# Token-major k, q and v of a gated-delta mixer by VectorE block transposes and scattered stores

## The chip, the cores and the metric

The kernel runs on one NeuronCore of one Trainium2 chip. The metric is the device time of one execution in microseconds; a lower number is better. The kernel before took 2305.7 us (median of 3 runs, 2305.63 to 2308.47).

The engines are named as the profile names them: PE (TensorE, matrix products) with its weight loads PEld, DVE (VectorE), ACT (ScalarE), POOL (GpSimd) and SP (SyncE, whose queue issues every DMA of this kernel). Each engine works through its own instructions in a fixed order and waits where an operand is not there yet.

## The reference

One layer of a hybrid encoder trunk, on a prompt of 2048 tokens and a sample of 32, width 1024, all in fp32:

- h = RMSNorm(x) with shift and scale from a conditioning vector, then one input projection whose columns feed two mixers.
- Mixer A: u and v through GELU, v normalised and mixed over 128-token chunks, out = u * (W v + b).
- Mixer B, the gated delta rule, is where the change lies. For each of 4 heads of 128 features:

```
qkv = silu(causal_conv(qkv, width 4))
q = l2norm(q) * 128 ** -0.5 ;  k = l2norm(k)
beta = sigmoid(b) ;  g = -exp(a_log) * softplus(a + dt_bias)
S_t = a_t S_{t-1} (I - b_t k_t k_t^T) + b_t v_t k_t^T ;  o_t = S_t q_t
```

  evaluated in chunks: a triangular system per chunk, products of q and k inside the chunk, and a state S of 128 x 128 that is carried from chunk to chunk.
- The mixers' outputs are joined and projected, added to x with a gate; then a feed-forward block of width 4096 with squared ReLU, and a final RMSNorm. Besides y, the last conv rows and the states S are returned.

## The kernel before

**Precision and layout.** A large product is three fp32r products of high and low parts (`mm3`): `BH`, `BL` are the parts of the activations, `wh`, `wl` those of the weights. Activations lie feature-major: 128 features on the partitions, tokens along the row. The prompt is worked in two halves (`hf`): 1024 tokens in two groups of 512, and 1056 tokens (with the sample) in groups of 384, 384 and 288.

**Stages of a half** (`mixers`, from about 90 us to 970 us): the v columns and gates of mixer A and the decays; then six weight slabs of two 128-column tiles each for k, q and v of the heads (z too in the second half); then u; then the output projection. During the first half's k/q/v slabs, `x_stats(1)` also makes the normalised input of the second half, with 48 loads of x and 24 stores and loads of h1.

**A k, q or v tile** (`qkv_tile`, L1146): each group accumulates 24 products in a bank of the ring `g`, ACT copies the bank to `raw`, DVE makes the conv with three more multiply-adds from `raw`, ACT applies SiLU, and the result is stored feature-major to DRAM: `kq_d` for k and q, `v_d` for v.

**A head** (`delta_local`, L1183) follows its v tile. For each pair of chunks (256 tokens, four pairs a half) it loads `kq` (ring `kq1`, slot 7) and `vt`, transposes k and q of both chunks on PE into a bank of the ring `L`, squares them on ACT with an accumulated sum for the norms, and copies k, scaled by the decay `ekg`, into the packet `pk`; POOL makes the power -1/2 of four sums. PE makes the products k with k and q in a second bank `L`, DVE multiplies them with the decays: one result goes to `pk`, the other stays as the triangular system. v is transposed in a third bank `L`, scaled and copied to `pk`, and `pk` (3 x 256 columns) is stored. `delta_inv` then inverts the triangular systems of two heads, and `delta_chain` runs the state over the eight chunks of two heads, loading `pk`, the inverse `us` and `kq` a pair ahead.

**What sets the order.** No order is written out by hand. Every operation is recorded with an engine, a cost, a class (chain, inversion, local work, evacuation, large product) and what it depends on, and `Program.schedule` places operations one at a time, engine by engine, by class and due time. On PE the large products fill the time in which smaller work is not ready. The outcome is a fixed list for each engine, in which nothing overtakes. A DMA's planned cost comes from its bytes; the argument `n` of `dma` gives another number of bytes to plan with.

**Helper lines.** Since helpers record everything, the profile's lines are those of the helpers: L358 activations, L373 `tt`, L378 `stt`, L387 `ts`, L396 copies, L404 the 32 x 32 block transpose of DVE, L411 every DMA, L420 every product, L431 every PE transpose. The tiles tell them apart: `g`, `L`, `C`, `B`, `M`, `f` are PSUM banks, `s` is any of the 28 SBUF slots. Names in the trace leave out digits, so `s<-kq_d` is a load of any head.

## Time and profile before

| | |
|---|---|
| median of 3 runs | 2305.7 us |
| profiled execution, its own time | 2305.26 us |
| profiled execution, its span from the first to the last instruction | 2303.5 us |
| mean granted clock of PE | 0.998 |
| PE busy, 180 to 980 us | 795.0 of 800 us |
| DMA busy share, whole span | 72.6% in the one queue that SP issues to |
| DMA traffic | 547 MB, 238 GB/s mean |

Feed-forward work fills the time from about 985 us on; the mixers with their projections lie before. In the first half the k/q/v tiles run from about 180 to 340 us, in the second from about 470 to 700 us. A busy PE in these views includes overlap between neighbouring instructions: starts tell how fast they follow each other.

### The profile page before, as it was taken

How to read it: one execution, taken by the hardware profiler on the slowest of the kernel's cores; microseconds unless marked ns; L12 is line 12 of the kernel's file. 1: busy time of each engine (PE TensorE's matmuls, PEld its weight loads, DVE VectorE, ACT ScalarE, POOL GpSimd, SP SyncE). 2: the span in 40 equal slices, each digit the busy share in tenths (PEclk: the TensorE clock that was granted, in tenths of full speed). 3: DMA queues.
4: the chain of work that ended last, by engine and by line, in shares of the span. 5: the costliest groups of instructions: out<-in, count | busy, mean ns of one | idle time of the engine just before them, and what ended most of it. 6: DMA issues, size and time to landing. Idle time of an engine off the chain costs nothing.

```text
span 2303.5 us, 45375 instructions
## 1 busy us (share of the span) xinstructions
PE 2280.8 (99%) x15890; PEld 2172.0 (94%) x15890; DVE 1660.0 (72%) x3599; ACT 1208.3 (52%) x2787; POOL 568.0 (25%) x722
## 2 busy tenths in 40 slices
PE   9999999999999999999999999999999999999998
PEld 6877879999999988999999999999999999999998
DVE  7556756677654546589999989876668885666775
ACT  5466656566654434476655546753444564344344
POOL 1123531222413023444445424210001250000001
PEclk9999999999999999999999999999999999999999
DMA  9578877576556857987777787997668797666771
GB/s 330 170 267 285 265 233 234 154 225 206 155 182 197 263 190 226 295 267 265 257 255 263 251 273 242 335 306 246 216 212 265 258 306 230 217 220 216 249 221 54
DMA packets 358198, 547.32 MB, mean 238 GB/s; under 512 B 66233, under 2 KB 182093, under 8 KB 357969
## 3 DMA queue, kind: packets, MB, share of 16 engines
q1 hardware_dynamic: 357968, 544.42, 72.6%
q8 instruction: 125, 2.05, 0.4%
q14 instruction: 105, 0.85, 0.1%
HBM read 390.96 MB, written 153.31 MB: 236 GB/s over the span
## 4 chain that ended last, share of the span: by engine, by line
PE 84%; DVE 6%; DMA 4%; ACT 2%; issue 2%; SPq 1%; POOL 1%; POOLq 0%; DVEq 0%; ACTq 0%
PE f L420 47%; PE g L420 27%; DVE s L373 4%; PE C L420 3%; PE B L420 2%; PE L L420 2%; DVE wl L373 1%; SPq L411 1%; ACT s L358 1%; PE M L420 1%; PE L L431 1%; DMA s<-x_d 1%; POOL s L373 0%; DMA s<-s_d 0%; ACT wh L358 0%
## 5 line engine op out<-in xcount | busy, mean ns | idle before, releaser
L420 PE MATMUL f<-s,wh 128*128 128x348 f32 (+1 forms) x2768 | 662.3, 322 | 1.3 <-DVE s L373 1.3
L358 ACT ACTIVATE s<-s 128x348 f32<-128x348 f32 (+13 forms) x1059 | 491.2, 487 | 326.6 <-DVE s L373 146.8
L420 PEld LDWEIGHTS f<-s,wh 128*128 128x128 f32 x2768 | 481.0, 188 | 3.3 <-DVE s L373 2.8
L373 DVE TENSOR_TENSOR s<-f,s 128x348 f32<-128x348 f32 (+1 forms) x696 | 348.0, 513 | 166.6 <-PE f L420 164.5
L420 PE MATMUL f<-s,wl 128*128 128x348 f32 (+1 forms) x1384 | 444.7, 321 | 0.0
L420 PE MATMUL g<-BH,wh 128*128 128x384 f32 (+2 forms) x1088 | 400.4, 368 | 2.4 <-ACT s L358 1.9
L373 DVE TENSOR_TENSOR s<-s,s 128x348 fp32r<-128x348 f32 (+8 forms) x674 | 353.2, 553 | 41.1 <-ACT s L358 20.5
L420 PE MATMUL g<-BH,wl 128*128 128x384 f32 (+2 forms) x1088 | 381.7, 351 | 0.0
L420 PE MATMUL g<-BL,wh 128*128 128x384 f32 (+2 forms) x1088 | 380.6, 350 | 0.5 <-DVE BL L378 0.5
L420 PE MATMUL f<-BL,wh 128*128 128x348 f32 (+1 forms) x1024 | 330.2, 322 | 0.0
L420 PE MATMUL f<-BH,wh 128*128 128x348 f32 (+1 forms) x1024 | 329.0, 321 | 0.0
L420 PE MATMUL f<-BH,wl 128*128 128x348 f32 (+1 forms) x1024 | 328.6, 321 | 0.0
L373 POOL TENSOR_TENSOR s<-s,s 128x512 f32<-128x512 f32 (+17 forms) x303 | 241.3, 800 | 341.2 <-ACT s L358 138.0
L358 ACT ACTIVATE wh<-s 128x512 fp32r<-128x512 f32 x282 | 176.6, 631 | 226.6 <-PE f L420 180.3
L420 PEld LDWEIGHTS f<-s,wl 128*128 128x128 f32 x1384 | 260.4, 188 | 0.0
L373 DVE TENSOR_TENSOR wl<-s,wh 128x512 fp32r<-128x512 f32 x282 | 217.2, 777 | 37.9 <-ACT wh L358 37.7
L420 PEld LDWEIGHTS g<-BH,wh 128*128 128x128 f32 x1088 | 204.9, 188 | 26.8 <-issue 7.1
L420 PEld LDWEIGHTS g<-BH,wl 128*128 128x128 f32 x1088 | 204.3, 188 | 18.2
L420 PEld LDWEIGHTS g<-BL,wh 128*128 128x128 f32 x1088 | 205.4, 189 | 16.6 <-DVE BL L378 0.8
L378 DVE SCALAR_TENSOR_TENSOR s<-s,s,s 128x256 f32<-128x256 f32 (+4 forms) x314 | 164.1, 544 | 55.3 <-ACT s L358 29.5
L358 ACT ACTIVATE wh<-wr 128x512 fp32r<-128x512 f32 (+2 forms) x159 | 124.3, 783 | 139.6 <-PE f L420 61.0
L420 PEld LDWEIGHTS f<-BL,wh 128*128 128x128 f32 x1024 | 192.3, 188 | 0.4 <-DVE BL L373 0.3
(134 smaller groups left out, 3264.6 us busy)
## 6 DMA issues: line engine op xcount, KB each, us to landing
s<-w_u SPq DMA_DIRECT2D x124, 256.0 KB, 3.6
s<-w_d SPq DMA_DIRECT2D x121, 256.0 KB, 3.9
wh<-su_d SPq DMA_DIRECT2D x114, 256.0 KB, 3.8
wl<-su_d SPq DMA_DIRECT2D x114, 256.0 KB, 4.1
wh<-sd_d SPq DMA_DIRECT2D x100, 256.0 KB, 3.0
wl<-sd_d SPq DMA_DIRECT2D x100, 256.0 KB, 3.8
wr<-w_b SPq DMA_DIRECT2D x36, 512.0 KB, 5.0
s<-adaw SPq DMA_DIRECT2D x32, 512.0 KB, 5.9
```

The lines of the kernel that those rows point to most:

```text
L358: self.p.op(ACT, c, lambda: nc.scalar.activation(out=R(out), in_=R(in_), func=func, **{k: R(v) for k, v in kw.items()}), [out, accum], [in ...
L373: self.p.op(eng, c, lambda: e.tensor_tensor(out=R(out), in0=R(a), in1=R(b), op=op), [out], [a, b])
L378: self.p.op(DVE, c, lambda: nc.vector.scalar_tensor_tensor(out=R(out), in0=R(a), scalar=R(s), in1=R(b), op0=op0, op1=op1), [out], [a, s, b])
L411: self.p.op(DMA, max(500, x), lambda: nc.sync.dma_start(out=R(out), in_=R(in_)), [out], [in_], lat=LAND + b / RATE - max(500, x))
L420: nc.tensor.matmul(R(out), R(l), R(r), **kw)
L431: self.p.op(PE, 114, lambda: nc.tensor.transpose(R(out), R(in_), R(ident)), [out], [in_, ident])
```

## The change

k, q and v of a tile are no longer transposed by PE. After the SiLU of a whole tile, kept in one buffer `yo` of 1056 columns, DVE transposes it in 32 x 32 blocks into `yt` (slot 8). The blocks are then brought into place by the store: for k and v one DMA writes `yt` to `kt_d`, token-major in DRAM, in 4 x 1056 pieces of 32 floats (128 bytes); its planned size is `9 * P * SLOT` bytes where its data are 4 x P x SLOT. For k and q, ACT squares `yt` in place, DVE sums each run of 32, and the partial sums go through DRAM (`ns_d`) to the start of the head's half, where one PE transpose, one sum and one power make the norms of all eight chunks.

The scaling of k by `ekg` and v by `nk` moves into the chain's loads, which now read `kt_d`, so `pk` holds only the masked product of q and k (256 columns where 768 were). Products of k and q in bank `L` stay as they are. The projection's ring `g` has three PSUM banks where it had two, `L` has one where it had two. The conv's last factor is read from `raw` in SBUF and not from the bank. The weights come as k q k q v v for each two heads, and `delta_local` follows the q tile. `x_stats` gets due times. The sample of 32 tokens reads the same new tensors. The core of the diff:

```diff
-        self.banks = {"g": [0, 1], "L": [3, 2], "C": [4, 5], "B": [6], "M": [7]}
+        self.banks = {"g": [0, 1, 2], "L": [3], "C": [4, 5], "B": [6], "M": [7]}
...
+        self.yt = self.slot(8, 0, (P, SLOT))
+        self.yo = self.slot(20, 0, (P, SLOT))
...
-        self.v_d = [dt(f"v_d{h}", [P, T]) for h in range(H)]
+        self.kt_d = [[dt(f"kt_d{h}_{f}", [SLOT, 2, P]) for f in range(2)] for h in range(H)]
+        self.ns_d = [[dt(f"ns_d{h}_{f}", [2, 4, SLOT]) for f in range(2)] for h in range(H)]
...
+            self.p.due = len(self.p.ops) + 300 * (g + 1)
...
-            fm = ["k0", "q0", "v0", "k1", "q1", "v1", "k2", "q2", "v2", "k3", "q3", "v3"]
+            fm = ["k0", "q0", "k1", "q1", "v0", "v1", "k2", "q2", "k3", "q3", "v2", "v3"]
...
-                        if name[0] == "v":
+                        if name[0] == "q":
                             self.delta(hf, int(name[1]))
+                        elif name[0] == "v":
                             due.append(int(name[1]))
...
-            self.act(y, ps, AF.Identity, scale=cw(3))
+            self.act(y, raw[:, 3 : 3 + w], AF.Identity, scale=cw(3))
...
             self.act(yo, y, AF.Silu)
-            self.dma(dst[:, T0[hf] + o : T0[hf] + o + w], yo)
+            if ty < 2:
+                self.dma(self.kq_d[h][:, 1 - ty, T0[hf] + o : T0[hf] + o + w], yo)
+        self.transpose32(self.yt.re("p (c j) -> p c j", j=32), self.yo.re("p (i c) -> p c i", i=32))
+        if ty:
+            self.dma(self.kt_d[h][hf][:, ty - 1].re("t (b j) -> b t j", b=4), self.yt, 9 * P * SLOT)
+        if ty < 2:
+            self.act(self.yt, self.yt, AF.Square)
+            part = self.new("sqp")
+            self.sums(part, self.yt.re("p (c j) -> p c j", j=32))
+            self.dma(self.ns_d[h][hf][1 - ty].re("b (i c) -> (b i) c", i=32), part)
+
+    def sums(self, out, in_):
+        nc = self.nc
+        self.p.op(DVE, 68 + 1.042 * in_.n, lambda: nc.vector.tensor_reduce(R(out), R(in_), AXIS.X, ALU.add), [out], [in_])
...
+        self.dma(ns[:64], self.ns_d[h][hf][:, :, :TW[0]].re("x b (c p) -> (x b) c p", p=P))
+        ss, rr = rr[:, :16], rr[:, 16:]
+        pt = self.bank("B")
+        self.tr(pt[:, :64], ns[:64], self.ident[:64, :64])
+        self.sums(ss.re("p (x c) -> p x c", x=2), pt[:, :64].re("p (x b c) -> p x c b", x=2, b=4))
+        self.ts(ss, ss, EPS, ALU.add)
+        self.rsqrt_small(rr, ss)
...
-            pt = self.bank("L")
-            for x in range(2):
-                for e in range(n):
-                    o = 256 * x + 128 * e
-                    self.tr(pt[:, o : o + 128], kq[:, x, wide(e)], self.ident)
-            for x in range(2):
-                for e in range(n):
-                    o = 256 * x + 128 * e
-                    jk = self.new("jk")
-                    self.act(jk[:w], pt[:w, o : o + 128], AF.Square, accum=ss[:w, n * x + e : n * x + e + 1])
...
-            pv = self.bank("L")
-            for e in range(n):
-                self.tr(pv[:, 128 * e : 128 * e + 128], vt[:, wide(e)], self.ident)
...
-            self.dma(self.pk_d[h][b], pk)
+            self.dma(self.pk_d[h][b], at)
...
+            self.dma(kv, self.kt_d[h][hf][lt : lt + W].re("(e p) x j -> p e (x j)", e=n))
+            self.dma(us, self.us_d[h][hf][:, P * lc : P * lc + W])
+            self.dma(at, self.pk_d[h][b])
             self.dma(kq, self.kq_d[h][:, :, t0 : t0 + W])
+            for e, c in enumerate(cl):
+                for x, k in enumerate((self.ekg, self.nk)):
+                    v = kv[:, e, P * x : P * x + P]
+                    self.act(v, v, AF.Copy, scale=k[:, h, c : c + 1])
```

**How it moves instructions.** PE, while the first half's k/q/v tiles are projected; before (`s_470` is `kq1`, `s_471` is `vt`, `C` is a bank of the chain's products):

```order
L420 MATMUL g_2370<-BH_71,wl 128x512
L431 MATMUL L_2411<-ident,s_471 128x128 x2
L420 MATMUL C_960<-s_476,s_465 128x128 x4
L431 MATMUL L_2435<-ident,s_470 128x128 x4
L420 MATMUL L_2450<-s_470 128x256 x2
L420 MATMUL g_2370<-BH_72,wh 128x512
L420 MATMUL g_2370<-BL_80,wh 128x512
```

and with the change (`s_482` is `kq1`, `s_481` holds the loaded sums of squares):

```order
L422 MATMUL g_2413<-BL_86,wh 128x512
L422 MATMUL g_2413<-BH_78,wl 128x512
L422 MATMUL L_2527<-s_482 128x256 x2
L433 MATMUL B_2461<-ident,s_481 128x64
L422 MATMUL g_2455<-BH_71,wh 128x512
L422 MATMUL g_2455<-BL_79,wh 128x512
```

The products of k and q stand alone now; a transpose of 64 columns in bank `B`, once for each half of a head, is the only one left of the norms.

SP's queue in the same stage, before, around a store of v (`s_484`, `s_485` take x, `s_469` is `pk`, `s_470` is `kq1`, `nd_d` takes the small blocks that the inversion starts from):

```order
L411 DMA pk_d_2_113<-s_469 128x768
L411 DMA s_484<-xT 128x384
L411 DMA v_d_102<-s_483 128x512
L411 DMA s_485<-xT 128x384 x2
L411 DMA s_470<-kq_d_98 128x2x256
L411 DMA s_484<-xT 128x384
L411 DMA nd_d_0_159<-s_468 16x8x16 x8
```

and with the change, around the scattered store of v of head 0 (`s_483` is `yt`, `s_496` takes x, `s_475` is the chain's packet):

```order
L413 DMA kt_d_0_101<-s_483 4x1056x32
L413 DMA s_482<-kq_d_98 128x2x256
L413 DMA pk_d_2_125<-s_481 128x256
L413 DMA s_500<-pk_d_1_124 128x256
L413 DMA s_496<-xT 128x384
L413 DMA wr_96<-w_b 128x1024
L413 DMA s_482<-kq_d_98 128x2x256
L413 DMA s_475<-kt_d_0_101 128x2x256
```

Behind the scattered store stand loads that PE's local products need (`kq_d`), the chain's packets and the next weights (`w_b`).

ACT, with the change, around the first square of a k tile:

```order
L360 ACTIVATE s_493<-g_2059 128x512
L360 ACTIVATE s_496<-s_496,modc,a_89 128x384
L360 ACTIVATE s_483<-s_483 128x1056
L360 ACTIVATE s_493<-g_2096 128x512
L360 ACTIVATE s_495<-s_494 128x512 x2
L360 ACTIVATE s_494<-s_493,s_492 128x512 x2
L360 ACTIVATE wh<-wr_96 128x1024
```

The square in place (`s_483`) must wait for the scattered store to have read `yt`, and the evacuation of the next projection bank (`s_493<-g`) and a half of the next weights' split stand behind it.

More of the change, by code (lines that the diff above doesn't have):

```diff
@@ L742, in startup @@
         stats(1, ())
-        zs = [self.bank(t) for t in "ggLL"]
+        zs = [self.bank(t) for t in "gggL"]
         for h in range(H):
@@ L1370, in sample @@
             self.act(n32, n32, AF.Exp)
[L1371 to L1376 removed]
+            self.sums(ss, ns.re("p (x b) -> p x b", x=2))
+            self.act(kg, kg, AF.Copy, scale=ekg)
             self.ts(ss, ss, EPS, ALU.add)
```

94 lines of the change are left out of this document (43 added, 51 removed).

## The prediction

> **What bounds the kernel now.** I read the page first: the share of each engine, the granted clock, and the chain that ended last (engines, then lines).
>
> ```profile
> span 2303.5 us, 45375 instructions
> PE 2280.8 (99%) x15890; PEld 2172.0 (94%) x15890; DVE 1660.0 (72%) x3599; ACT 1208.3 (52%) x2787; POOL 568.0 (25%) x722
> PEclk9999999999999999999999999999999999999999
> PE 84%; DVE 6%; DMA 4%; ACT 2%; issue 2%; SPq 1%; POOL 1%; POOLq 0%; DVEq 0%; ACTq 0%
> PE f L420 47%; PE g L420 27%; DVE s L373 4%; PE C L420 3%; PE B L420 2%; PE L L420 2%; DVE wl L373 1%; SPq L411 1%; ACT s L358 1%; PE M L420 1%; PE L L431 1%; DMA s<-x_d 1%; POOL s L373 0%; DMA s<-s_d 0%; ACT wh L358 0%
> ```
>
> TensorE is busy 99% of the span at full clock, and 84% of the chain is its own work; `f` is the feed-forward part, which the change leaves alone. The transposes to be removed are the `L L431` entry, 1% of the chain. Next the stretches between 180 and 980 us, which hold the mixers' projections and chains, and TensorE's waits from 150 to 720 us (total, times, longest):
>
> ```profile
> 180.00:340.00 160.00, 159.49 (x1126) 129.14 (x1125) 105.90 (x239) 99.04 (x276) 66.24 (x111) 1.00 0.83 265
> 340.00:470.00 130.00, 129.85 (x1378) 121.72 (x1376) 85.57 (x286) 72.64 (x214) 28.16 (x57) 1.00 0.66 201
> 470.00:700.00 230.00, 227.06 (x1882) 221.37 (x1881) 148.94 (x477) 136.38 (x433) 63.17 (x163) 1.00 0.61 190
> 700.00:980.00 280.00, 278.61 (x2060) 256.49 (x2059) 156.97 (x360) 118.22 (x265) 85.42 (x121) 1.00 0.75 235
> ```
> ```profile
> PE g L420 <- ACT s L358: 1.9, 3, 0.9
> PE L L431 <- ACT s L358: 1.0, 1, 1.0
> PE B L420 <- DVE s L396: 0.5, 1, 0.5
> ```
>
> The columns are length, then busy time of PE, PEld, DVE, ACT and POOL, clock, DMA share and GB/s. TensorE idles 5.0 us in 800 (0.51+0.15+2.94+1.39), and never for a DMA, although the 16 DMA engines are at 0.83 in the first projection stretch. So time taken off TensorE here is time off the kernel, as long as nothing takes the place of what is removed.
>
> **What the change takes from TensorE.** All 195 transposes into bank L go (6 for each of 32 pairs of chunks, 3 for the sample), and 8 of the norms come, one for each half of a head.
>
> ```profile
> L431 PE MATMUL L<-ident,s 128*128 128x128 f32 x195 | 28.8, 274 | 1.0 <-ACT s L358 1.0
> ```
> ```profile
> 264.78 0.39 PE L420 MATMUL g<-BH,wl 128*128 128x512 f32 x1
> 265.01 0.82 PE L431 MATMUL L<-ident,s 128*128 128x128 f32 x6
> 265.58 0.48 PE L420 MATMUL g<-BH,wh 128*128 128x512 f32 x1
> 265.90 0.40 PE L420 MATMUL g<-BL,wh 128*128 128x512 f32 x1
> ...
> 268.22 0.39 PE L420 MATMUL g<-BH,wl 128*128 128x512 f32 x1
> 268.45 1.03 PE L420 MATMUL L<-s 128*128 128x256 f32 x4
> 269.12 0.59 PE L420 MATMUL g<-BH,wh 128*128 128x512 f32 x1
> 269.55 0.39 PE L420 MATMUL g<-BL,wh 128*128 128x512 f32 x1
> ```
>
> The group's busy time is 28.8 us, 0.148 us for each, but neighbours overlap, so I go by starts. Products follow each other every 0.23 us (264.78 to 265.01). From the first of six transposes (265.01) to the second product behind them (265.90) are 0.89 us; less one product that is 0.66, or 0.11 us a transpose. Net 187 of them: **20.6 us**; by the busy time it would be 27.7. I take the starts. The fp32 products of q and k (268.45) stay, and cost the next product 0.43 - 0.23 = 0.20 us for the change of kind; the new order has 182 places where fp32 work breaks into the projection against 190, so 8 × 0.2 = **1.6 us** more. A third bank for projections and one for L replace two and two: bounded by the 1.9 us that TensorE waits for `g` evacuation, and taken as nothing.
>
> **What it gives to the others**, by these groups (busy us, mean ns):
>
> ```profile
> L404 DVE STREAM_TRANSPOSE s<-s 128x512 f32<-128x512 f32 x8 | 5.7, 709 | 3.1 <-DMA s<-ud_d 3.0
> L373 DVE TENSOR_TENSOR wl<-wr,wh 128x1024 fp32r<-128x1024 f32 x52 | 65.7, 1264 | 37.5 <-ACT wh L358 35.8 <-DMA z_d<-s 1.3
> L373 DVE TENSOR_TENSOR s<-s 128x2 f32<-128x2 f32 x128 | 19.2, 176 | 21.5 <-POOL s L373 19.2 <-ACT s L358 1.9
> L358 ACT ACTIVATE s<-L 128x128 f32<-128x128 f32 x130 | 36.6, 281 | 4.5 <-PE L L431 3.0
> L358 ACT ACTIVATION_READ_ACCUMULATOR s<-L 128x1 f32 x130 | 27.1, 209 | 0.0
> L358 ACT ACTIVATE s<-L,s 128x128 f32<-128x128 f32 x130 | 41.5, 366 | 27.8 <-PE L L431 15.3 <-DMA pk_d<-s 12.3
> L358 ACT ACTIVATE s<-s 128x1024 f32<-128x1024 f32 x8 | 8.5, 1062 | 0.9 <-DVE s L378 0.9
> L373 POOL TENSOR_TENSOR s<-s,mhalf 128x4 f32<-128x4 f32 x32 | 34.6, 1081 | 94.3 <-DVE s L387 92.1 <-DVE s L378 2.0
> ```
>
> VectorE: 24 block transposes of 1056 columns, 709 × 1056/512 = 1.46 us each (upper bound; 1.30 by the 1024-wide row), 35 us. 16 sums over 1056 columns: no row has one; between half of and all of the 1264 ns row scaled to 1056 (0.65 to 1.30), I take 1.30 as it is read one element at a time there too, 21 us. 160 tiny operations of 0.17 us go and 48 come: -19. Net **+37 us** in 390 us of projection stretches where it is busy 255. ScalarE: squares (36.6) and their accumulator reads (27.1) go; the 130 scaled copies stay, moved to the chain's loads, now from SBUF (366 ns bounds them); 16 squares of 1056 columns at 1.1 us come: **-46 us**. Gpsimd: 32 powers of four columns become 8 of sixteen, each between today's 1.1 us and four times that: 9 to 34 us against 34.6. None of these engines is near full, so in bulk they are hidden; if that cover went, 37 us of VectorE would be the price.
>
> What is late next is a road: last product of a k tile, conv and SiLU, transpose (1.46), scattered store, square (1.1), sum (1.3), store and load of the sums, transpose in bank B, and only then `ck`. `yt` and `yo` are single buffers, so the next tile's transpose waits for the store (k, v) and the sum (k, q). The square of k stands in ScalarE's order ahead of projection evacuations; three `g` banks are the cover, two tiles' groups of 24 × 0.23 = 5.6 us.
>
> **The scattered stores.** 16 of 4224 pieces of 128 bytes (528 KB). The nearest transfer is the load from `ud_d`, 2048 pieces of 128 bytes:
>
> ```profile
> s<-ud_d SPq DMA_DIRECT2D x4, 256.0 KB, 4.0
> nd_d<-s SPq DMA_DIRECT2D x64, 8.0 KB, 1.6
> pk_d<-s SPq DMA_DIRECT2D x32, 384.0 KB, 3.0
> s<-pk_d SPq DMA_DIRECT2D x32, 384.0 KB, 4.0
> ```
> ```profile
> 311.00:312.00 1.00, 1.00 (x6) 0.82 (x5) 0.96 (x4) 0.98 (x2) 0.90 (x2) 1.00 1.01 350
> ```
>
> It lands in 4.0 us where 128 tiny pieces land in 1.6, so 2.4 us for 2048 and 5.0 for 4224: a store lands in 6.6 us and holds the queue 5.0 at most; at least 1.5, its bytes at the 350 GB/s of the full stretch shown. In the first stretch 8 stores hold 40 us at most. Free there are 0.17 × 160 = 27 us, plus what goes: the stores and loads of v (4.2 MB) and two thirds of the `pk` stores (4.2 MB), 32 us at 265 GB/s, less 10 us by which the stretch shortens: 49 us. They fit. In the second, 0.39 × 230 = 90 and more are free.
>
> The store's target is walked with 4 (the 32-feature blocks) as outermost count, against 128 partitions on the other side; `ud_d` has 128 on both. No row of the trace tells on how many engines a transfer ran. The Trainium skill (DMA: Bandwidth & Descriptors, "Why a DMA increments its semaphore by 16 and not by 1") states that a transfer uses the largest number up to 16 that divides the outermost counts of both sides. By that it would be four here, and rival C's sum would stand instead of the one below; by the `ud_d` row it is the sum below.
>
> **The sum.** The profiled execution took 2305.26 us (span 2303.5), 0.4 below the median of 2305.7. 2305.3 - 20.6 - 1.6 = 2283.1. For new waits on the longer roads I put as much again as TensorE idles in these 800 us today, +5.0, between -5.0 (today's waits go too) and +16 (each of 16 stores once holds TensorE 1 us): 2288, and **2289 us** against the median; 2279 to 2299 for this case.
>
> **Rivals.** *B: the norm road takes the place of what is removed.* Each half-head's `ck` waits for square and sum behind the store, 1.1 + 1.3 = 2.4 us; if bank B's transpose, fixed in TensorE's order, meets that eight times, 19 us return: about 2303. For it: TensorE's order cannot swap. Against: today's squares, powers and scales stand 32 times in the same engines' orders, and TensorE's waits for those engines add up to the three rows above, 3.4 us.
>
> *C: the store runs on a quarter of the engines, and is slower than what it replaces.* If the queue splits work by the outermost count 4, a store holds four engines for 6.2 (bytes at a quarter of 350 GB/s) to 19.8 us (4 × 5.0), everything behind it in SP's queue lands no earlier, and a k store that lands at 12 or more holds ScalarE's square with the evacuations behind it. I take the geometric middle, 11 us. First stretch: 8 × 11 = 88 against 49 free, 39 over, and weights, q/k loads and chain loads stand in that queue. Second: 88 fits, with 1 us of TensorE waiting for each store, 8. So 2283.1 + 47 + 0.4, about **2331 us**; at 19.8, 109 over and 34 over, up to 2427; at 6.2 it merges with B. It decides from about 9 us a store (8 × 9 = 72, 23 over the 49 free, against 22.2 saved). The page's rule above is this mechanism. Against C: TensorE kept its pace at a DMA share of 0.94:
>
> ```profile
> 205.00:225.00 20.00, 20.00 (x99) 16.49 (x98) 14.17 (x39) 13.51 (x39) 7.71 (x11) 1.00 0.94 324
> ```
>
> The change not doing what it says is excluded on TensorE: no transpose into L is left in its order.
>
> **How the numbers follow.** Forecast 0.47; B 0.12; C 0.38 (nothing in the trace excludes the split, and the page speaks for it; but it costs time only past the cover); 0.03 for anything else. Same means within 0.2% (2301 to 2310), which is what a measurement of this kernel can tell. Faster 0.48, same 0.12, slower 0.40. The range starts at 2281 and reaches into C to 2337, past its middle; about 0.17 lies above, 0.03 below.
>
> **What would show it.** Right: TensorE's busy time down by 20 to 28 us, its idle time from 180 to 980 us near 10, stores to `kt_d` landing in 5 to 8 us. B: waits of bank B's transposes for VectorE or ScalarE of 2 us, eight times. C: stores to `kt_d` landing in 12 us or more; waits of TensorE for DMA, or for ScalarE behind a square, that add up to over 20 us. The forecast fails if projections wait for evacuation although three banks rotate.

## The result: 5.5% slower

The changed kernel takes 2433.4 us (median of 4 runs, 2432.5 to 2438.6) against 2306.1 for the kernel before in the same session: a ratio of 1.055, 95% interval 1.054 to 1.057. The forecast was 2289 us, the range 2281 to 2337. The profiled execution took 2433.43 us, its span is 2431.7. Its page: span, TensorE, the granted clock in 40 slices, the chain by engine and by line.

```profile
span 2431.7 us, 44648 instructions
PE 2303.1 (95%) x15703; PEld 2178.7 (90%) x15703; DVE 1706.5 (70%) x3528; ACT 1197.9 (49%) x2548; POOL 555.4 (23%) x699
PEclk9998888999988999999999999999999999999999
PE 77%; DMA 10%; DVE 5%; ACT 3%; SPq 2%; issue 2%; POOL 1%; POOLq 0%; DVEq 0%; ACTq 0%
PE f L422 50%; PE g L422 20%; DMA kt_d<-s 3%; PE C L422 3%; SPq L413 2%; PE B L422 2%; ACT s L360 2%; DVE s L375 2%; DVE s L380 2%; PE L L422 1%; DMA wr<-w_b 1%; DVE s L406 1%; PE M L422 1%; POOL s L375 1%; DMA s<-xT 1%
```

The transposes are gone (187 TensorE instructions fewer), and yet TensorE is busy 22.3 us longer. It is idle 2431.7 - 2303.1 = 128.6 us where it was idle 22.7. So the 128.2 us of span are 105.9 of new waiting and 22.3 of products that ran longer. Nearly all of it lies in the two stretches of the k, q and v tiles, where TensorE idles 111.6 us instead of 5.0 and the granted clock is 0.89 and 0.93 instead of 1.00. Windows of the kernel before (first fence) and of the changed one:

```profile
180.00:470.00 290.00, 289.34 (x2500) 250.85 (x2499) 191.47 (x524) 171.68 (x490) 94.39 (x168) 1.00 0.75 236
470.00:860.00 390.00, 385.67 (x3229) 365.36 (x3228) 235.76 (x717) 201.84 (x598) 101.91 (x245) 1.00 0.64 202
```
```profile
180.00:470.00 290.00, 234.14 (x1526) 190.94 (x1526) 166.87 (x318) 118.24 (x234) 74.99 (x108) 0.89 0.65 179
470.00:860.00 390.00, 334.29 (x2875) 318.81 (x2874) 237.38 (x653) 184.93 (x450) 87.00 (x230) 0.93 0.57 153
```

In the first, TensorE does 1526 products where it did 2500, every engine is busy for less, and the DMA engines move 179 GB/s instead of 236. SyncE's queue tells why. These are its DMA issues (start, duration) around three of the 16 scattered stores:

```profile
213.84 0.57 SPq L413 DMA_DIRECT2D kt_d<-s  x1
214.51 12.33 SPq L413 DMA_DIRECT2D pk_d<-s  x1
...
276.24 0.59 SPq L413 DMA_DIRECT2D kt_d<-s  x1
276.92 14.03 SPq L413 DMA_DIRECT2D kq_d<-s  x2
...
298.94 0.57 SPq L413 DMA_DIRECT2D kt_d<-s  x1
299.55 15.14 SPq L413 DMA_DIRECT2D s<-xT  x1
```

The store itself is issued in 0.6 us; what is issued behind it is held 12.3 to 15.1 us. Behind 14 of the 16 stores the next issue comes within 2 us, and those were held 11.6 to 16.2 us, the middle 12.5. In that time the DMA engines do almost nothing else. These windows of 5 us have the columns of the prediction's windows; the two from 215 to 225 us lie inside the first hold shown:

```profile
195.00:200.00 5.00, 0.00 (x0) 0.00 (x0) 0.99 (x1) 1.57 (x2) 0.19 (x1) 0.74 0.75 201
200.00:205.00 5.00, 4.96 (x13) 2.63 (x14) 3.14 (x4) 2.60 (x5) 0.00 (x0) 0.58 1.04 374
205.00:210.00 5.00, 5.00 (x26) 4.07 (x25) 5.00 (x7) 2.79 (x4) 2.15 (x3) 1.00 1.05 355
...
215.00:220.00 5.00, 5.00 (x23) 4.05 (x22) 4.57 (x8) 3.36 (x6) 0.53 (x1) 1.00 0.27 44
220.00:225.00 5.00, 5.00 (x24) 4.03 (x23) 1.88 (x5) 0.00 (x0) 0.67 (x1) 1.00 0.36 45
...
295.00:300.00 5.00, 5.00 (x13) 3.87 (x12) 2.26 (x5) 2.44 (x6) 0.00 (x0) 0.52 0.95 290
300.00:305.00 5.00, 5.00 (x23) 4.06 (x22) 3.38 (x7) 2.78 (x9) 1.34 (x2) 1.00 0.63 187
```

A DMA share of 0.27 to 0.36 and 44 to 45 GB/s: about a quarter to a third of the 16 engines' time. The store's 540,672 bytes at 45 GB/s are 12.0 us, which is the hold. The same windows show the second loss. After a stall of 5.2 us (195 to 200, no product; it ended with a load of `adaw`, and SyncE had been held 16.2 us on such a load behind the first store) TensorE is busy all the time, but starts 13 products in 5 us at a granted clock of 0.58, and 26 in the next 5 us at 1.00; the same at 295 us, behind a stall of 8.1 us (13, then 23). So a stall is paid again, with 4 to 5 us at about half pace: large products start every 0.43 us there, and every 0.23 behind it. The Trainium skill (TensorE: Matmul & The Clock Gate, "Part 1: The HAM clock gate") says that the array's clock is halved after an idle window of about 3.4 us and comes back after as long a busy one; the halving agrees with these rows, and the return took 4 to 5 us here.

Who waits for the store: ScalarE's squares and VectorE's next block transposes, and what stands behind them in their orders. The three largest waits of TensorE in the changed kernel (total, times, longest), and the groups that the change brought (busy, mean ns, idle before):

```profile
PE B L422 <- DVE s L406: 24.1, 2, 15.8
PE C L422 <- DVE s L380: 19.8, 8, 7.7
PE L L422 <- DMA s<-kq_d: 13.1, 3, 8.2
```
```profile
L406 DVE STREAM_TRANSPOSE s<-s 128x1056 f32<-128x1056 f32 x24 | 51.3, 2136 | 29.7 <-DMA kt_d<-s 25.5 <-ACT s L360 4.0
L1193 DVE TENSOR_REDUCE s<-s 128x33 f32<-128x1056 f32 x16 | 20.0, 1249 | 45.3 <-ACT s L360 45.3
L360 ACT ACTIVATE s<-s 128x1056 f32<-128x1056 f32 x16 | 17.2, 1077 | 65.6 <-DMA kt_d<-s 53.0 <-issue 10.0 <-DVE s L406 2.5
L375 POOL TENSOR_TENSOR s<-s,mhalf 128x16 f32<-128x16 f32 x8 | 23.9, 2981 | 21.7 <-DVE s L389 17.3 <-ACT s L360 4.0 <-DVE s L375 0.4
```

ScalarE stood 53.0 us before its 16 squares until a store had been read out of `yt`, and VectorE 25.5 us before its block transposes. TensorE's own waits are spread over many names: those for DMAs add up to some 33 us, those for evacuations of projection banks to 7.0.

### The profile page after: what moved, and what is told of

The parts are those of the page before. It is cut to its first block, busy times and chain, and to the rows that moved or that the text cites. A ratio compares the mean times of both kernels' runs of the same rounds, so it can differ in the third digit from the quotient of the medians.

```text
span 2431.7 us, 44648 instructions
## 1 busy us (share of the span) xinstructions
PE 2303.1 (95%) x15703; PEld 2178.7 (90%) x15703; DVE 1706.5 (70%) x3528; ACT 1197.9 (49%) x2548; POOL 555.4 (23%) x699
## 4 chain that ended last, share of the span: by engine, by line
PE 77%; DMA 10%; DVE 5%; ACT 3%; SPq 2%; issue 2%; POOL 1%; POOLq 0%; DVEq 0%; ACTq 0%
PE f L422 50%; PE g L422 20%; DMA kt_d<-s 3%; PE C L422 3%; SPq L413 2%; PE B L422 2%; ACT s L360 2%; DVE s L375 2%; DVE s L380 2%; PE L L422 1%; DMA wr<-w_b 1%; DVE s L406 1%; PE M L422 1%; POOL s L375 1%; DMA s<-xT 1%
## 5 line engine op out<-in xcount | busy, mean ns | idle before, releaser
L360 ACT ACTIVATE s<-s 128x348 f32<-128x348 f32 (+14 forms) x1075 | 505.7, 495 | 402.0 <-DVE s L375 141.3
L422 PE MATMUL g<-BH,wh 128*128 128x384 f32 (+2 forms) x1104 | 414.8, 376 | 7.5 <-ACT s L360 7.0
L422 PE MATMUL g<-BL,wh 128*128 128x384 f32 (+2 forms) x1104 | 395.2, 358 | 0.5 <-DVE BL L380 0.5
L422 PE MATMUL g<-BH,wl 128*128 128x384 f32 (+2 forms) x1104 | 394.6, 357 | 0.0
L375 POOL TENSOR_TENSOR s<-s,s 128x512 f32<-128x512 f32 (+16 forms) x303 | 242.1, 804 | 398.0 <-ACT s L360 178.9
L422 PEld LDWEIGHTS g<-BH,wh 128*128 128x128 f32 x1104 | 214.2, 194 | 35.6 <-issue 8.0
L422 PEld LDWEIGHTS g<-BH,wl 128*128 128x128 f32 x1104 | 213.1, 193 | 20.7 <-DVE wl L375 0.3
L422 PEld LDWEIGHTS g<-BL,wh 128*128 128x128 f32 x1104 | 213.8, 194 | 17.9 <-DVE BL L380 0.8
L422 PEld LDWEIGHTS f<-BH,wh 128*128 128x128 f32 x1024 | 192.6, 188 | 1.5 <-ACT wh L360 1.0
L422 PEld LDWEIGHTS f<-BH,wl 128*128 128x128 f32 x1024 | 193.0, 188 | 0.2 <-DMA wl<-su_d 0.2
```

The costliest lines, as they stand in the source:

```text
L360: self.p.op(ACT, c, lambda: nc.scalar.activation(out=R(out), in_=R(in_), func=func, **{k: R(v) for k, v in kw.items()}), [out, accum], [in ...
L375: self.p.op(eng, c, lambda: e.tensor_tensor(out=R(out), in0=R(a), in1=R(b), op=op), [out], [a, b])
L422: nc.tensor.matmul(R(out), R(l), R(r), **kw)
```

## The experiments

Medians in us; the ratio is to the kernel before in the same session (2304.5 to 2307.0), with its 95% interval.

| kernel | time | ratio |
|---|---|---|
| after the change | 2433.4 | 1.054 to 1.057 |
| store in four, 32 partitions each | 2389.1 | 1.032 to 1.037 |
| the same, contiguous pieces | 2384.6 | 1.032 to 1.035 |
| store in two | 2647.3 | 1.145 to 1.150 |
| store from ScalarE's queue | 2462.3 | 1.065 to 1.070 |
| four, planned with true sizes | 2383.7 | 1.033 to 1.037 |
| ... no norms | 2322.8 | 1.006 to 1.010 |
| ... banks 2 and 2 | 2390.9 | 1.036 to 1.040 |
| ... two tile buffers | 2375.5 | 1.029 to 1.032 |
| ... norms made, not read | 2378.5 | 1.029 to 1.033 |
| ... two tile buffers, measured costs planned | 2373.7 | 1.027 to 1.031 |
| ... not read, no squares | 2370.3 | 1.026 to 1.030 |
| ... not read, no sums | 2355.0 | 1.019 to 1.023 |
| ... no norms, q turned | 2356.2 | 1.020 to 1.024 |
| ... two turned-tile buffers | 2331.8 | 1.009 to 1.013 |
| ... and the old order of tiles | 2322.6 | 1.006 to 1.009 |
| ... and squares on Gpsimd (new order) | 2342.7 | 1.015 to 1.018 |
| before, new order alone | 2315.8 | 1.002 to 1.005 |
| before, v alone turned | 2306.7 | 0.999 to 1.001 |

### Is it the store, and what in it?

The theories and rivals named in this part by letters (A, B, C, then P, R, L) are those of the expectations; the prediction's rivals B and C are others.

**Four stores.** One store with 4 as the outermost count of its target becomes four with 32 on both sides. Pieces and places stay.

```diff
-            self.dma(self.kt_d[h][hf][:, ty - 1].re("t (b j) -> b t j", b=4), self.yt, 9 * P * SLOT)
+            kt = self.kt_d[h][hf][:, ty - 1].re("(i c) f -> i c f", i=32)
+            for b in range(4):
+                q = slice(32 * b, 32 * b + 32)
+                self.dma(kt[:, :, q], self.yt[q].re("p (c j) -> p c j", j=32), 9 * 32 * SLOT)
```

> Each scattered store is cut into four, one for each block of 32 features; every piece of 128 bytes and its place stay as they are, but each of the four is walked with 32 as the outermost count on both sides instead of 4 on one side and 128 on the other. Theory A (the whole store ran on 4 of the 16 DMA engines because 4 is the outermost count of its target): the 11.6 to 16.2 us for which the transfer behind each store was held fall to about a quarter, 3 to 4 us, TensorE's idle time falls from 128.6 us to under 45, and the time to 2275 to 2300 us. Rival B (4224 pieces of 128 bytes are slow on however many engines): the hold stays at 11 to 16 us and the time at 2420 to 2440. Rival C (the store is not what costs; the third bank, the new order of the tiles or the road of the norms is): the hold falls but the time stays over 2400.

2389.1 us, 44 below the change. The hold is gone: these are SyncE's issues around the four parts of one store, and the second row is a plain store behind the first part.

```profile
219.19 0.56 SPq L413 DMA_DIRECT2D kt_d<-s  x1
219.85 0.60 SPq L413 DMA_DIRECT2D kq_d<-s  x1
...
223.37 0.61 SPq L413 DMA_DIRECT2D kt_d<-s  x1
224.08 2.05 SPq L413 DMA_DIRECT2D s<-kq_d  x2
...
226.81 0.59 SPq L413 DMA_DIRECT2D kt_d<-s  x1
...
230.17 0.59 SPq L413 DMA_DIRECT2D kt_d<-s  x1
```

What follows a part now takes 0.6 us, or 2.05 for two. So theory A is right on the hold, and wrong on the time: 2275 to 2300 was expected, and 82 us over the kernel before stay. TensorE is still idle for 2388.7 - 2294.6 = 94.1 us, where under 45 was expected. The four parts are issued some 4 us apart, 11 us from the first to the last.

**Contiguous pieces.** The same four stores, each partition's 4224 bytes in one run.

```diff
-            kt = self.kt_d[h][hf][:, ty - 1].re("(i c) f -> i c f", i=32)
+            kt = self.kt_d[h][hf].re("(i c) x f -> i (c x f)", i=32)
...
-                self.dma(kt[:, :, q], self.yt[q].re("p (c j) -> p c j", j=32), 9 * 32 * SLOT)
+                o = 4 * SLOT * (ty - 1) + SLOT * b
+                self.dma(kt[:, o : o + SLOT], self.yt[32 * b : 32 * b + 32], 9 * 32 * SLOT)
```

> The same four stores of 32 partitions and the same bytes, but each partition's 4224 bytes go to one contiguous run of the target. This changes the order of k and v in memory, so what is computed from them is changed; every instruction of the engines stays. Theory A: the small pieces cost little once 16 engines share them, so this is within 10 us of the kernel with four scattered stores, both 2275 to 2300. Rival B (the pieces of 128 bytes are the cost): this one alone falls to 2275 to 2300, and the one with four scattered stores stays over 2400. Rival C (the rest of the change costs): this one too stays over 2400.

2384.6 us, 4.5 below the scattered four, and the ranges of their runs overlap. The size of the pieces is worth next to nothing once 32 stands outermost on both sides; rival B falls. Rival C's figure, over 2400, is not met either, but most of it stands: something else in the change costs some 80 us.

**Two stores.** Two blocks of 32 features each, the outermost count 2.

```diff
+            kt = self.kt_d[h][hf][:, ty - 1].re("t (b j) -> b t j", b=4)
+            for b in range(2):
+                self.dma(kt[2 * b : 2 * b + 2], self.yt[64 * b : 64 * b + 64], 9 * 64 * SLOT)
```

> Each scattered store is cut into two, of two blocks of 32 features each, so that the outermost count of the target is 2 instead of 4. Theory A (engines follow the outermost count): each half has as many pieces for each engine as the whole has now (1056) on two engines, so the transfers behind are held for 23 to 32 us for a pair instead of 11.6 to 16.2, unless the halves run beside each other; with 16 stores and 8 to 16 us more of waiting for TensorE at each, 2520 to 2680 us. Rival B (so many pieces, whatever the engines): 2425 to 2445, as after the change.

2647.3 us, within theory A's range. Each half, with half the pieces, holds the queue as long as the whole did:

```profile
181.04 0.59 SPq L413 DMA_DIRECT2D kt_d<-s  x1
181.73 15.68 SPq L413 DMA_DIRECT2D s<-adaw  x1
...
200.43 0.54 SPq L413 DMA_DIRECT2D kt_d<-s  x1
201.07 14.19 SPq L413 DMA_DIRECT2D h_d<-s  x2
```

Of the 32 issues behind a half, 27 were held 12.2 to 15.7 us. A window inside the hold from 250.20 to 262.39 us:

```profile
252.00:261.00 9.00, 4.65 (x16) 3.57 (x16) 0.24 (x2) 0.39 (x1) 4.01 (x3) 0.84 0.18 22
```

22 GB/s, half of the 44 behind a whole store. Other windows inside the halves' holds lie at 25 GB/s and more, where other transfers are still under way; windows inside the whole stores' holds lie at 43 to 58. Half the bytes take the same time, and a quarter of the bytes (four stores) hold nothing: time and rate go with the outermost count, as if 2, 4, and 16 engines worked where it is 2, 4, and 32 on both sides. No row counts the engines themselves.

**Another queue.** The store whole, from ScalarE's queue.

```diff
-            self.dma(self.kt_d[h][hf][:, ty - 1].re("t (b j) -> b t j", b=4), self.yt, 9 * P * SLOT)
+            out, yt = self.kt_d[h][hf][:, ty - 1].re("t (b j) -> b t j", b=4), self.yt
+            self.p.op(DMA, 500, lambda: self.nc.scalar.dma_start(out=R(out), in_=R(yt)), [out], [yt], ...)
```

> The scattered store is left whole, but ScalarE's queue issues it instead of SyncE's, so that the transfers behind it in SyncE's queue no longer stand behind it in the same queue. If the cost is the place in the queue alone: the loads of weights, q, k and chains pass it, and the time falls to 2285 to 2320 us. If the cost is that 4 of the 16 engines are taken and every other transfer needs a part from those 4: it stays between 2400 and 2440, with the transfers issued behind a store landing 8 to 15 us later than others.

2462.3 us, above both ranges. SyncE's queue is no longer held (what it issues next behind the 16 stores takes 0.3 to 0.65 us), but the store is as long, and ScalarE, whose next work is the square of the same buffer, waits for it. ScalarE's rows behind two stores, with the idle time before them in brackets:

```profile
205.07 1.08 ACT L360 ACTIVATE s<-s 128x1056 f32<-128x1056 f32 x1 [12.93 <-DMA kt_d<-s]
...
239.92 1.08 ACT L360 ACTIVATE s<-s 128x1056 f32<-128x1056 f32 x1 [14.18 <-DMA kt_d<-s]
```

So another place does not help a store that stays as long: its length is paid there too. Whether the transfers beside it landed later, this run's trace does not tell.

### What is left with the store mended?

Every run from here on, but for the two that start from the kernel before, has the store in four, planned with its true bytes.

```diff
-                self.dma(kt[:, :, q], self.yt[q].re("p (c j) -> p c j", j=32), 9 * 32 * SLOT)
+                self.dma(kt[:, :, q], self.yt[q].re("p (c j) -> p c j", j=32), 4 * 32 * SLOT)
```

> The store in four parts as before, but the planner that writes the order counts their true bytes (4 a value) instead of 9 a value. With 9 it reckons 3.4 us of queue for each part, and in the run the four parts of one tile were issued 4 us apart (219.19, 223.37, 226.81, 230.17 us) though each took the queue 0.6 us. Theory P (what was left over the kernel before, 82 us, comes from an order made for a slow store): the four parts are issued within 3 us, the transposes' buffer comes free some 10 us earlier, and the time falls to 2283 to 2315 us. Rival R (the road itself: one buffer for the transposed tile and one for the tile, passed by transpose, store, square and sum): 2350 to 2390. Rival L (one bank L instead of two holds the chunk work): 2350 to 2390.

2383.7 us, 5 below the four stores planned with 9 bytes a value, with intervals that overlap. This is a weak test of theory P. The 3.4 us in the expectation are what the plan reckons for a whole store (`schedule` divides bytes by 350); a part counts 0.87 us with 9 bytes a value and 0.39 with 4. So the edit moves little: the parts of a store are still issued over 9.4 to 50.7 us, first to last, in the middle 12, where theory P expected 3. The true bytes are worth 5 us; an order that issues the four parts together was not tried. This kernel is the base of what follows, and TensorE's largest wait in it is for ScalarE's evacuations of projection banks, with three banks in the ring:

```profile
PE g L422 <- ACT s L360: 33.7, 12, 11.3
```

**Without norms.**

```diff
-        self.transpose32(self.yt..., self.yo...)
-        if ty:
+        if ty:
+            self.transpose32(self.yt..., self.yo...)
             ...
         if ty < 2:
-            self.act(self.yt, self.yt, AF.Square)
-            part = self.new("sqp")
-            self.sums(part, self.yt.re("p (c j) -> p c j", j=32))
-            self.dma(self.ns_d[h][hf][1 - ty].re("b (i c) -> (b i) c", i=32), part)
+            self.dma(self.ns_d[h][hf][1 - ty].re("b (i c) -> (b i) c", i=32), self.cst)
```

> As the kernel with true sizes, but the squares, their sums and the transposes of q are left out; the sums of squares that the chunks load are a constant, so the norms of k and q are not computed. Theory P: within 15 us of the kernel with true sizes. Rival R: at least 30 us below it, 2270 to 2310. Rival L: within 15 us of it.

2322.8 us, 61 below the base: rival R's size.

**Banks 2 and 2.** `"g": [0, 1], "L": [3, 2]`, as before the change.

> As the kernel with true sizes, with two banks for projections and two for L as before the change. Theory P and rival R: within 15 us of the kernel with true sizes, rather slower by up to 15, since an evacuation of a projection that comes late then stops TensorE one tile earlier. Rival L: 30 us or more below it.

2390.9 us, 7 above the base, with intervals that overlap. Rival L falls; the third bank for projections helps a little at most.

**Two tile buffers.** The SiLU works in place in one of two buffers of 1056 columns (slots 19 and 20).

```diff
-            raw, y, yo = self.new("raw"), self.half("y", w), self.yo[:, o : o + w]
+            raw, y = self.new("raw"), yo[:, o : o + w]
...
-            self.act(yo, y, AF.Silu)
+            self.act(y, y, AF.Silu)
```

> As the kernel with true sizes, with two buffers for the tile of 1056 columns: the SiLU writes in place, so the two slots that held halves of its input and output now hold two whole tiles, and the SiLU of the next tile need not wait for the transpose of this one. Theory P: within 10 us of the kernel with true sizes, both below 2315. Rival R: ScalarE's waits for the transposes (60.9 us, 19 times, from 150 to 850 us with four stores) fall by half or more and the time by 20 to 60 us against true sizes alone. Rival L: within 10 us of the kernel with true sizes, both over 2350.

2375.5 us, 8 below the base, between what was expected of P or L (within 10) and of R (20 or more). The tile buffer ahead of the transpose is not the main narrow place.

**Norms made, not read.** All the work stays; the chunks load a constant, so nothing waits for its result.

```diff
-        self.dma(ns[:64], self.ns_d[h][hf][:, :, :TW[0]].re("x b (c p) -> (x b) c p", p=P))
+        self.dma(ns[:64], self.cst_d)
```

> As the kernel with true sizes: transposes of q, squares, sums and stores of the sums are all made, but the chunks load constants in place of those sums, so that nothing waits for them; the norms used are not those of k and q. Leaving the norms out altogether was worth 61 us (2383.7 to 2322.8). Road theory (the chunks' work waits for transpose, square, sum, store and load): 2318 to 2335 us. Work theory (the squares, sums and transposes stand in ScalarE's and VectorE's orders and hold the one buffer of the transposed tile, whoever reads them): 2365 to 2390.

2378.5 us: the road from the norms to the chunks is worth 5 us, the work of making them, 56.

**Costs as measured in the plan.** Block transposes and powers planned with their traced durations, on the kernel with two tile buffers.

```diff
-        self.p.op(DVE, 68 + 1.042 * out.n, lambda: nc.vector.transpose(...), [out], [in_])
+        self.p.op(DVE, 68 + (2.0 if out.n > 1000 else 1.25) * out.n, lambda: nc.vector.transpose(...), [out], [in_])
...
-            c = 300 + 165 * n
+            c = 300 + (220 if n > 8 else 185) * n
```

> As the kernel with two tile buffers, but the planner counts what the trace showed for a block transpose of 1056 columns (2.18 us in place of 1.17), for one of 512 (0.71 in place of 0.60) and for a power of 16 columns (3.83 us in place of 2.94). If orders made for too fast a road are what makes TensorE wait: 20 us or more below 2375, down to 2320. If the road is too long wherever it is planned: 2365 to 2380.

2373.7 us, 2 below its base. Planning the road better does not shorten it.

### Which part of the norms' work?

**No squares; no sums; only q's transposes.** In the first the turned tile is summed unsquared, in the second the partial sums are a constant (both with the norms not read). The third adds to the kernel without norms the transposes of q, which nobody reads.

```diff
-            self.act(self.yt, self.yt, AF.Square)
```
```diff
-            self.sums(part, self.yt.re("p (c j) -> p c j", j=32))
```
```diff
-        if ty:
-            self.transpose32(self.yt..., self.yo...)
+        self.transpose32(self.yt..., self.yo...)
+        if ty:
```

> As the kernel whose norms are made but not read (2378.5), without the 16 squares on ScalarE: the turned tile is summed as it is. If ScalarE's order, in which a square waits for the transpose with projection evacuations behind it, holds TensorE: 25 us or more lower, 2325 to 2353. If it is VectorE's share: 2365 to 2380.

> As the kernel whose norms are made but not read (2378.5), without the 16 sums on VectorE; the squares are made and nobody reads them. If VectorE's share is what holds TensorE: 25 us or more lower, 2325 to 2353. If it is ScalarE's squares: 2365 to 2380.

> As the kernel without norms (2322.8), but q's tiles are turned again by VectorE and nobody reads them: 8 transposes of 2.18 us more, each through the one buffer of the turned tile. If the transposes of q and their place in the buffer are the cost: 2340 to 2378. If it is the squares and sums behind them: 2318 to 2330.

2370.3 (8 less), 2355.0 (24 less) and 2356.2 (33 more than without norms). No part carries the cost by itself: neither run reached 25 us, and q's transposes alone bring back more than half of it. What the parts have in common is `yt`.

**Two buffers for the turned tile.** The second is slot 19, which held the halves of the SiLU's input; the SiLU works in place in the one tile buffer.

```diff
-        rg("y", hv(19), (P, 512))
-        self.yt = self.slot(8, 0, (P, SLOT))
+        self.yts = [self.slot(s, 0, (P, SLOT)) for s in (8, 19)]
...
+        self.yts.reverse()
+        yt = self.yts[0]
```

> As the kernel with true sizes, with two buffers for the turned tile (the second in the slot that held the input halves of the SiLU, which now works in place), so that the next tile's transpose need not wait for this one's store, square and sum. Buffer theory (one turned tile is the narrow place): 20 us or more below 2383.7, down to 2325. Work theory (what matters is that squares, sums and transposes stand in the orders of ScalarE and VectorE): 2370 to 2390.

2331.8 us, 52 below the base, with every square, sum and transpose in place: the buffer theory. The SiLU in place is part of this edit; it was in the two tile buffers' kernel too, which gained 8. ScalarE's waits for block transposes from 180 to 860 us and the first stretch, in the base (first two rows) and here (last two):

```profile
ACT s L360 <- DVE s L406: 59.2, 21, 6.5
```
```profile
180.00:470.00 290.00, 255.36 (x1939) 210.81 (x1939) 189.86 (x408) 138.15 (x306) 84.61 (x145) 0.92 0.71 203
```
```profile
ACT s L360 <- DVE s L406: 32.6, 16, 3.4
```
```profile
180.00:470.00 290.00, 268.27 (x2190) 227.52 (x2189) 203.42 (x454) 152.31 (x343) 86.18 (x151) 0.97 0.74 208
```

TensorE does 2190 products there instead of 1939, at a clock of 0.97 instead of 0.92. A tile of the first half keeps TensorE for 48 × 0.23 = 11.0 us. The four steps of a k tile in `yt` are short: transpose 2.14, a part's landing 3.5 (the median where the base's trace gives one), square 1.08, sum 1.25, together 8.0.

```profile
kt_d<-s SPq DMA_DIRECT2D x64, 132.0 KB, 3.5
```

But they do not follow each other at once. The base's rows for one k tile, from the three engines:

```profile
215.50 2.15 DVE L406 STREAM_TRANSPOSE s<-s 128x1056 f32<-128x1056 f32 x1
217.68 0.56 SPq L413 DMA_DIRECT2D kt_d<-s  x1
...
229.57 0.59 SPq L413 DMA_DIRECT2D kt_d<-s  x1
234.18 1.07 ACT L360 ACTIVATE s<-s 128x1056 f32<-128x1056 f32 x1
235.45 1.25 DVE L1196 TENSOR_REDUCE s<-s 128x33 f32<-128x1056 f32 x1
```

From 215.50 to the end of the sum at 236.70 are 21.2 us, 11.9 of them between the first and the last of the store's four parts, with other transfers issued between. Over the base's eight k tiles it is 20.3 to 30.0 us, for a q tile, which has no store, 5.1 to 14.0. So one k tile holds the buffer for about two tiles' time of TensorE, and the next transpose comes late.

### The rest

**The order of tiles.** Alone, in the kernel before (first diff line), and undone, in the kernel with two turned-tile buffers (the reverse).

```diff
-            fm = ["k0", "q0", "v0", "k1", "q1", "v1", "k2", "q2", "v2", "k3", "q3", "v3"]
+            fm = ["k0", "q0", "k1", "q1", "v0", "v1", "k2", "q2", "k3", "q3", "v2", "v3"]
```

> The kernel before the change with the order of the tiles alone (k, q of two heads, then their v). If the order costs nothing: 2298 to 2312 us. If it is the order that is left when the norms are taken out (2322.8 against the 2289 forecast): 2320 to 2345.

> As the kernel with two buffers for the turned tile (2331.8), with the tiles in the order of before (k, q, v of one head after another). If the new order costs in the mended kernel what it cost alone (10 us): 2316 to 2326. If it is needed there, since a head's chunk work now starts at its q tile and the new order brings the second q forward by a tile: 2330 to 2350.

2315.8 us alone, between the two sizes expected (10 us more than before, ratio 1.002 to 1.005); 2322.6 undone, 9 less than with it. The order costs 9 to 10 us in either kernel. In the kernel before a head's chunk work follows v, and in the changed one q, so both runs need not have the same cause; which wait carries it was not followed up.

**Squares on Gpsimd.**

```diff
-            self.act(yt, yt, AF.Square)
+            self.tt(yt, yt, yt, ALU.mult, POOL)
```

> As the kernel with two buffers for the turned tile (2331.8), with the 16 squares on Gpsimd instead of ScalarE. If ScalarE's order is what is left (TensorE waits 24.8 us for it, 11 times): 2308 to 2325. If VectorE's order sets when a projection's evacuation can go, or Gpsimd is too slow (over 2 us a square): 2328 to 2350.

2342.7 us, 11 more: a square takes 2.19 us there instead of 1.08, and holds the turned tile longer.

**v alone.** In the kernel before, v goes by block transposes, one group of tokens at a time in two buffers, with the store in four; k, q, norms, order and banks stay.

```diff
-            self.dma(dst[:, T0[hf] + o : T0[hf] + o + w], yo)
+            if ty < 2:
+                self.dma(self.kq_d[h][:, 1 - ty, T0[hf] + o : T0[hf] + o + w], yo)
+                continue
+            yt = self.half("yt", w)
+            self.transpose32(yt.re("p (c j) -> p c j", j=32), yo.re("p (i c) -> p c i", i=32))
+            kt = self.kt_d[h][hf][o : o + w].re("(i c) f -> i c f", i=32)
+            for b in range(4):
+                q = slice(32 * b, 32 * b + 32)
+                self.dma(kt[:, :, q], yt[q].re("p (c j) -> p c j", j=32))
...
-                self.tr(pv[:, 128 * e : 128 * e + 128], vt[:, wide(e)], self.ident)
```

> The kernel before the change with only v turned by VectorE, half a tile at a time in two buffers, stored in four parts each walked from 32 partitions, and scaled when the chain loads it; k, q, their transposes and norms, the order of the tiles and the banks stay. 65 transposes leave TensorE, 65 x 0.11 = 7.2 us. If a transposed tile with a store on all engines is free as such: 2293 to 2303 us, faster than before. If transposes on VectorE and stores of small pieces stop TensorE by themselves: 2310 to 2340.

2306.7 us against 2305.9 (ratio 0.999 to 1.001): no difference, and neither range was met. The page, then the TensorE transposes that stay and one form of the new block transposes, by groups:

```profile
span 2306.0 us, 45331 instructions
PE 2277.0 (99%) x15825; PEld 2166.3 (94%) x15825; DVE 1675.7 (73%) x3619; ACT 1209.5 (52%) x2786; POOL 567.3 (25%) x722
```
```profile
L431 PE MATMUL L<-ident,s 128*128 128x128 f32 x130 | 20.2, 276 | 1.6 <-ACT s L358 1.5
L404 DVE STREAM_TRANSPOSE s<-s 128x384 f32<-128x384 f32 x8 | 7.0, 877 | 1.9 <-ACT s L358 1.7
```

65 transposes are gone, 7.2 us by the prediction's price; TensorE's busy time fell by 3.8, and its idle time rose from 22.7 to 29.0. Even this mildest part gives back what it takes.

No version beat the kernel before. The best that keeps the whole change, mended in the store, the buffer and the order, takes 2322.6 us, 16 over it. The page of its profiled execution (2326.9 us) and TensorE's largest wait there:

```profile
span 2325.1 us, 44774 instructions
PE 2275.0 (98%) x15703; PEld 2160.3 (93%) x15703; DVE 1705.5 (73%) x3528; ACT 1192.6 (51%) x2544; POOL 550.3 (24%) x699
```
```profile
PE g L422 <- ACT s L360: 16.9, 7, 5.8
```

Against the kernel before, TensorE is busy 5.8 us less there and idle 27.4 us more (50.1). The largest wait is again for ScalarE's evacuations. Why these waits remain is open: a third buffer for the turned tile, a second one for the tile beside the two, or the four parts of a store issued together were not tried.

## Why the prediction was wrong

**The step that failed first: "a store lands in 6.6 us and holds the queue 5.0 at most".** It was priced by the `ud_d` row, whose 128 partitions stand on both sides. The stores with 4 outermost held the queue 11.6 to 16.2 us; with 32 on both sides the hold vanished, with 2 it stayed as long for half the bytes. This is the Trainium skill's rule (DMA: Bandwidth & Descriptors, "Why a DMA increments its semaphore by 16 and not by 1"), which the prediction stated and gave up in favour of the `ud_d` row. That row could not speak against it, since by the rule its transfer has 16 engines. Rival C named the mechanism, with 6.2 to 19.8 us a store and a middle of 11; measured was 12.5. What spoke against C, TensorE keeping its pace at a DMA share of 0.94, was no evidence on a store in whose hold the share is some 0.3 to 0.4 at 44 GB/s. Its upper sum, 2427, is 6 us from the result, but by luck: it stands on 19.8 us a store, and taking the hold away gave only 2433.4 - 2383.7 = 50 us.

**The step that failed second: "+5.0 for new waits".** With the hold gone the time is still 95 us above the forecast. The prediction named the road and that `yt` is a single buffer, and then priced the road by today's waits, as if the same work on the same engines waited alike. A second buffer gives 52 of the 95; with one, a k tile held it 20.3 to 30.0 us, where TensorE makes a tile in 11.0. The prediction had counted bulk (VectorE 37 us in 390, "hidden"), and what filled was not an engine but a slot. Rival B (2303) put the price on the reading of the norms at bank B; with the reading cut off, in the base, 5 us went.

**The order of the tiles had no term but the 8 interruptions fewer (1.6 us saved); it costs 9 to 10 us.** The banks, taken as nothing, are worth 7 at most, in favour of the change.

**The clock was in no term.** The sum took each wait at its own length. Of the 128.2 us, 22.3 are longer busy time although the transposes left: with the 22.2 us that the prediction saw saved, 44 us of products at a lower clock; with the smaller saving that v alone shows, less. This is an estimate; the windows' clock (0.89 over 290 us, 0.93 over 390) bounds it by 0.11 × 290 + 0.07 × 390 = 59, part of which falls on idle time.

**The saving itself, 20.6 us by starts, is doubtful:** v alone brought 3.8 of its 7.2 in busy time, and no run settles why.

**Sizes that were off without deciding.** A block transpose of 1056 columns takes 2.14 us, above the "upper bound" of 1.46 scaled from a 512-column one (0.71); VectorE rose by 46.5 us in place of 37. The sum at 1.25 (1.30 foreseen), the square at 1.08 (1.1) and the power of 16 columns at 2.98 (1.1 to 4.3) were right. ScalarE's busy time fell by 10.4, not 46; one part of the difference is that the squares and their accumulator reads overlap in time, 48.5 us together where 63.7 were added up. Two slips in the sums decide nothing: 24 × 0.23 is 5.5, not 5.6, and the "34 over" of C's second stretch implies 124 us free, where only "90 and more" is written.

Of the signs named beforehand, both of C's came: TensorE's waits for DMAs add up to some 33 us, and the holds show stores of about 12 us. None of "right" did, and B's eight waits of bank B's transposes did not. The last sign, projections that wait for evacuation although three banks rotate, is small in the changed kernel (7.0 us) and the largest wait of TensorE once the store is mended (33.7).

## What to carry to other kernels

Read the outermost count of both sides of a transfer before its bytes: four stores of 32 partitions did not hold the queue that one store in four blocks held for 12 to 16 us. When work moves off the bound engine, follow the buffer that passes through the new steps, and compare the time from its first write to its last read with the time in which the next tile arrives. The steps' durations alone, 8.0 us against 11, would have passed; with the gaps between them it was 21 us for a k tile, and the one buffer cost 52. And price a stall of a few us of TensorE above its length, because the products behind it run at half pace.

## What the runs showed of the hardware

- The time of a transfer follows the outermost count of its two sides: holds of 12.2 to 15.7 us for half a store with count 2 (the lowest rate inside one 22 GB/s), 11.6 to 16.2 for a whole one with count 4 (the lowest 43), none with 32.
- 128-byte pieces against contiguous runs of 4224 bytes: 2389.1 against 2384.6 us, with 32 outermost on both sides.
- After stalls of TensorE of 5.2 and 8.1 us, 13 products in 5 us at a granted clock of 0.52 to 0.58, then 23 to 26 at 1.00.
- A block transpose of 1056 columns of fp32 takes 2.14 us, of 512 columns 0.71: three times as long for twice the columns. The 1056 are read with a stride of 33, the 512 without one. The stride counts by itself: in the kernel with v alone turned, 512 columns read with a stride of 16 take 1.05 to 1.08 us (8 of them), and 512 without one 0.70 to 0.72 (8 of them); 384 with a stride of 12 take 0.88.
